# Attention scores from stacked high and low parts, and softmax work moved to ScalarE, in a two-layer hybrid encoder

## The chip, the cores and the metric

The kernel runs on one core of a Trainium2 chip. The core has TensorE (PE, the matrix unit; PEld in the profile is its loading of stationary operands), VectorE (DVE), ScalarE (ACT), GpSimd (POOL) and a queue that issues the transfers (SP). The metric is the device time of one execution in microseconds.

## The reference

```
for l in range(2):
    x = layer_norm(ALPHA*x + 0.5*swiglu_1(x));  x = layer_norm(ALPHA*x + mixer(x));  x = layer_norm(ALPHA*x + 0.5*swiglu_2(x))

mixer(x):                                  # x: 256 tokens x 1024
    sc_b, sc_c, sc_h, q, k, v, cc_a, cc_gate = split(x @ w_in)
    y_sc  = sc_b * dwconv3(sc_c * sc_h)
    q, k  = rope(q), rope(k)               # 8 query heads, 2 key/value heads, 64 columns each
    s     = q @ k.T / 8, where |i-j| <= 128, else -1e30
    m     = max(max(s), sink);  p = exp(s - m)
    y_att = (p @ v) / (sum(p) + exp(sink - m))
    y_cc  = silu(layer_norm(dwconv31(cc_a * sigmoid(cc_gate)) + b))
    return concat(y_sc, y_att, y_cc) @ w_out
```

All inputs and the output are float32.

## The kernel before

**Precision.** The large matmuls run in fp32r, a float32 form of less precision. Each operand is kept as a high part (the value rounded to fp32r, a ScalarE copy) and a low part (value minus high part, a subtraction on VectorE or GpSimd); `split` makes the two. A product is the sum of three matmuls, high-high, high-low and low-high (`mm3`). The attention's own matmuls, the scores and the product with v, and the transposes use plain float32 operands instead; the trace shows two matmul records for each float32 score matmul.

**Order.** The text of the kernel gives a program order. A scheduler then places each engine's instructions at compile time, by that order and by what it estimates to be ready; an engine runs its own list in the order that results. In the last part of the mixer (`in_order`) GpSimd's instructions keep the written order. Weights come in blocks of 128x2048: one DMA each, then a split. Blocks 7 to 11 of a mixer and the first four of the next feed-forward part have their subtractions on GpSimd.

**The mixer.** Tokens form two tiles t of 128. After the projections for the gated convolution, queries are projected (`proj_n`), rotated (`rotate`) and turned by four transposes per tile into qT[t] (`q_turned`, lines 538 to 543): partitions 0 to 63 hold the heads that use key head 0, partitions 64 to 127 those that use key head 1. Keys go the same way, one transpose per tile, into kT (128 x 256, `k_turned`). Values stay in vn. The long convolution is 62 taps on VectorE (`emit_conv`, line 572), handed out in portions by `fill(n)` between other work.

Softmax works on four units u: token tile u // 2, and half i = u % 2 of the heads, four heads at a time. For each unit
- `scores` (line 581) takes two PSUM banks of the pool acc (four banks) and computes for each c and each j a 64-row score matmul, on the partitions of key head j; then it adds the mask by a bf16 matmul with the identity;
- `exps` (592) takes maxima on VectorE, nm = -max, four exponentials on ScalarE with nm as bias and a summed output, and es = exp(sink + nm) by an addition on VectorE and one 128x4 exponential;
- `normalise` (608) adds es to the sums, inverts them and scales the probabilities on ScalarE;
- `p_turned` (616) transposes the probabilities and copies the two banks out, one on ScalarE (623), one on VectorE (625);
- `attend` (629) multiplies by v into one scratch bank (`tmp_bank`, four banks in this phase) and splits the result into y[i].

Around them run the remaining projections `proj_c`, 24 matmuls of 256 columns each per half (psc, psh, psb for the gated convolution), as the text below the functions lists: psc's first half, then turned queries and keys, psc's second half with the first scores inside it, and so on to the output projection `w_out2`. y[0] to y[3] are pairs of tiles (high, low) for the mixer's output; y[2] is written late by the gated convolution, y[3] by the Conformer part.

Of the kernel before, what the change touches and what calls it, by code (L numbers as in the profile page):

```python
# [8 lines left out]
F32 = mybir.dt.float32  # L9
F32R = mybir.dt.float32r  # L10
BF16 = mybir.dt.bfloat16
AF = mybir.ActivationFunctionType
ALU = mybir.AluOpType
# [3 lines left out]
P = 128  # L17
D = 1024
S = 256
# [3 lines left out]
KC = D // P  # L23
NG = DFF // 256
HD = 64
# [22 lines left out]
def encoder(ctx: ExitStack, tc: tile.TileContext, head_in, xt_in, x_in, w_in, gb_in, small_in, rope_in, out):  # L48
    nc = tc.nc
# [9 lines left out]
    mx = pool("mx", 1)  # L59
# [15 lines left out]
    def big():  # L75
        return hpool.tile([P, 512], F32, tag="big", bufs=6, name="big")
# [4 lines left out]
    def bank():  # L81
        return acc.tile([P, 512], F32, tag="acc", name="bank")
# [10 lines left out]
    def tmp_bank():  # L93
        return phase["pool"].tile([P, 512], F32, tag="mm", name="tmp")
# [58 lines left out]
    def use(k):  # L153
        i = state["use"]
        state["use"] += 1
        return tuple(t.rearrange("p (k n) -> p k n", k=k) for t in blocks.pop(i))

    def release(delay=2):
        tasks.append((state["tick"] + delay, emit_block))

    def fill(n):
        for _ in range(min(n, len(conv))):
            conv.pop(0)()

    def tick(parts=1):
        state["tick"] += 1
        while tasks and tasks[0][0] <= state["tick"]:
            tasks.pop(0)[1](parts)

    def mm3(ps, ah, al, bh, bl, first, last):  # L170
        nc.tensor.matmul(ps, ah, bh, start=first, stop=False)  # L171
        nc.tensor.matmul(ps, ah, bl, start=False, stop=False)  # L172
        nc.tensor.matmul(ps, al, bh, start=False, stop=last)  # L173

    def proj_c(ps, w, c, ks=range(KC)):
        cs = slice(c * P, (c + 1) * P)
        for k in ks:
            mm3(ps[:, c * S:(c + 1) * S], w[0][:, k, cs], w[1][:, k, cs], xT_h[:, k], xT_l[:, k], k == 0, k == KC - 1)
        if k == KC - 1:
            if c == 1:  # L180
                release()
            tick()
# [13 lines left out]
    def proj_n(ps, t, w, kh):  # L196
        for k in range(4):
            kk = kh * 4 + k
            nc.tensor.matmul(ps, xT_h[:, kk, t, :], w[0][:, k, :], start=kk == 0, stop=False)  # L199
            nc.tensor.matmul(ps, xT_h[:, kk, t, :], w[1][:, k, :], start=False, stop=False)  # L200
        for k in range(4):
            kk = kh * 4 + k
            nc.tensor.matmul(ps, xT_l[:, kk, t, :], w[0][:, k, :], start=False, stop=kk == KC - 1)  # L203
        if t == NT - 1:
            release()
        tick()
# [14 lines left out]
    def transpose(ps, srcs):  # L221
        for i, a in enumerate(srcs):
            nc.tensor.transpose(ps[:, i * P:(i + 1) * P], a, ident)  # L223
# [273 lines left out]
    def mixer(l, norm):  # L497
# [3 lines left out]
        b_cc, gb_cc, sink = sm[:, 68:70], sm[:, 70:74], sm[:, 74:82]  # L501
# [7 lines left out]
        nc.gpsimd.memset(upad, 0.0)  # L509
        ppad = mx.tile([P, 2, S + 2], F32, tag="ppad", name="ppad")  # L510
        nc.gpsimd.memset(ppad, 0.0)
        kT = mx.tile([P, S], F32, tag="kT", name="kT")
        half = HD // 2
        chan = lambda a: a.rearrange("p (c n) -> p c n", c=2)

        def rotate(t, src, n):
            src = src.rearrange("p (h d) -> p h d", d=HD)
            rf, r2f = big(), big()
            r, r2 = (a[:, 0:n * HD].rearrange("p (h d) -> p h d", d=HD) for a in (rf, r2f))
            bc = lambda a: a.unsqueeze(1).to_broadcast([P, n, a.shape[-1]])  # L520
            nc.vector.tensor_tensor(r, src, bc(rope[:, t, 0, :]), ALU.mult)
            nc.vector.tensor_tensor(r2[:, :, 0:half], src[:, :, half:HD], bc(rope[:, t, 1, 0:half]), ALU.mult)
            nc.vector.tensor_tensor(r2[:, :, half:HD], src[:, :, 0:half], bc(rope[:, t, 1, half:HD]), ALU.mult)
            nc.vector.tensor_tensor(r, r, r2, ALU.add)
            return rf

        def glu(ps):
            tg, u = big(), big()
            nc.scalar.activation(tg[:, 0:256], ps[:, 0:256], AF.Tanh, scale=0.5)
            nc.vector.scalar_tensor_tensor(u[:, 0:256], tg[:, 0:256], 1.0, ps[:, 256:512], op0=ALU.add, op1=ALU.mult)  # L530
            return u
# [3 lines left out]
            transpose(pt, [u[:, 0:P], u[:, P:2 * P]])  # L535
            nc.scalar.copy(upad[:, :, PAD + t * P:PAD + (t + 1) * P], chan(pt[:, 0:2 * P]))

        def q_turned(r):
            pq = tmp_bank()
            transpose(pq, [r[:, c * P:(c + 1) * P] for c in range(4)])  # L540
            q = mx.tile([P, 4, P], F32, tag="qT", bufs=2, name="qT")
            nc.scalar.copy(q.rearrange("p c n -> p (c n)"), pq)
            return q

        def k_turned(t, r):
            pk = tmp_bank()
            transpose(pk, [r[:, 0:P]])
            nc.scalar.copy(kT[:, t * P:(t + 1) * P], pk[:, 0:P])

        def kv(t, w):  # L550
            ps = tmp_bank()
            for k in range(KC):
                mm3(ps[:, 0:256], xT_h[:, k, t, :], xT_l[:, k, t, :], w[0][:, k, :], w[1][:, k, :], k == 0, k == KC - 1)
            v = mx.tile([P, P], F32, tag="vn", bufs=2, name="vn")
            nc.scalar.copy(v, ps[:, P:2 * P])
            r = rotate(t, ps[:, 0:P], 2)
            if t == 1:
                release()
            tick()
            return v, r  # L560
# [18 lines left out]
        y = [[hpool.tile([P, 2, S], F32R, tag=n, bufs=5, name="y" + n) for n in ("hh", "hl")] for _ in range(4)]  # L579

        def scores(t, i):
            mo = 1 - t
            scs = [chan(bank()) for _ in range(2)]
            for c in range(2):
                for j in range(2):
                    hp = slice(j * HD, (j + 1) * HD)
                    nc.tensor.matmul(scs[j][:, c, :], qT[t][hp, 2 * i + c, :], kT[hp, :], start=True, stop=False)
                for j in range(2):
                    nc.tensor.matmul(scs[j][:, c, mo * P:(mo + 1) * P], ident_b, mask[:, t, :], start=False, stop=True)
            return scs  # L590

        def exps(i, scs):
            hs = slice(4 * i, 4 * i + 4)
            den, mxs, nm, es = (st.tile([P, 4], F32, tag=n, name=n) for n in ("den", "mxs", "nm", "es"))
            pr = mx.tile([P, 4, S], F32, tag="pr", bufs=2, name="pr")
            for j in range(2):
                nc.vector.tensor_reduce(mxs[:, j::2], scs[j], AX.X, ALU.max)  # L597
            nc.vector.scalar_tensor_tensor(nm, mxs, -0.125, nsink[:, hs], op0=ALU.mult, op1=ALU.min)
            nc.vector.tensor_tensor(es, sink[:, hs], nm, ALU.add)
            for j in range(2):  # L600
                for c in range(2):
                    h = 2 * c + j
                    nc.scalar.activation(pr[:, h, :], scs[j][:, c, :], AF.Exp, bias=nm[:, h:h + 1], scale=0.125,
                                         accum_out=den[:, h:h + 1])
            nc.scalar.activation(es, es, AF.Exp)
            return pr, den, es

        def normalise(pr, den, es):
# [7 lines left out]
        def p_turned(pr):  # L616
            pTs = []
            for j in range(2):
                pp = bank()
                transpose(pp, [pr[:, 2 * c + j, kt * P:(kt + 1) * P] for kt in range(NT) for c in range(2)])  # L620
                pT = big()
                if j == 0:
                    nc.scalar.copy(pT, pp)
                else:
                    nc.vector.tensor_copy(pT, pp)
                pTs.append(pT)
            return pTs

# [43 lines left out]
        qT, vn, rk = [], [], []  # L672
        ga, q = bank(), bank()
# [6 lines left out]
        r0 = rotate(0, q, NH)  # L680
        ga, q = bank(), bank()
        proj_n(ga, 1, wga[0], 0)
        glu_turned(0, u0)
        proj_n(ga, 1, wga[1], 1)
        u1 = glu(ga)
        qT.append(q_turned(r0))
        proj_n(q, 1, wq[0], 0)
        glu_turned(1, u1)
        cacc = emit_conv()
# [2 lines left out]
        r1 = rotate(1, q, NH)  # L692
        wkv = use(KC)
        v, rk0 = kv(0, wkv)
        vn.append(v)
        fill(6)
        v, rk1 = kv(1, wkv)
        vn.append(v)
        psc = tmp_bank()
        wc = use(KC)  # L700
        fill(6)
        proj_c(psc, wc, 0)
        qT.append(q_turned(r1))
        k_turned(0, rk0)
        k_turned(1, rk1)
        prs, pTs = {}, {}

        def softmax(u, scs):
            prs[u] = exps(u % 2, scs)

        def S_(u):
            return scores(u // 2, u % 2)
# [8 lines left out]
            normalise(*prs[u])  # L721

        fill(5)
        proj_c(psc, wc, 1, range(4))
        softmax(0, S_(0))
        proj_c(psc, wc, 1, range(4, KC))
        scc = big()
        nc.scalar.copy(scc, psc)
        fill(9)
# [30 lines left out]
        scs = S_(3)  # L760
# [59 lines left out]
    for l in range(DEPTH):  # L820
        norm = ffn(l == 0, norm, False)
        norm = mixer(l, norm)
        norm = ffn(False, norm, l == DEPTH - 1)
# [85 lines left out]
```

## Time and profile before

| | |
|---|---|
| median of 3 runs | 932.67 us (932.43 to 933.49) |
| profiled execution | 932.76 us, span of its instructions 931.0 us |
| granted TensorE clock | 0.997 of 2.4 GHz |
| busy | PE 919.6, DVE 643.6, ACT 457.6, POOL 120.9 us |
| the two mixers' softmax stretches | about 225 to 262 and 684 to 722 us |

The span runs from the first to the last instruction of the profiled execution; the rest of the time lies around it. Busy shares are means over stages with different limits, so a stage is read from its own stretch. Matmuls overlap: their starts tell more than their durations.

### The profile page before, as it was taken

Reading aid. Unit: us, or ns where it says so; the run is one execution under the profiler, and the core shown is the slowest. Engines: PE = TensorE matmul, PEld = TensorE weight load, DVE = VectorE, ACT = ScalarE, POOL = GpSimd, SP = SyncE. Lnnn points to the kernel's source line nnn. Section 1 sums busy time; section 2 is a strip of 40 time slices with the busy share of each in tenths; the row PEclk is TensorE's granted clock in tenths of the full one; section 3 lists DMA queues with packets and bytes.
Section 4 is the critical chain, followed back from the end, with each engine's and each line's share of the span. In section 5 each row is a group of like instructions: output and inputs, shape, how many; then the busy total and the mean of one; then the engine's idle time right before and its main releaser. Section 6 shows DMA issues by size and latency. Waiting matters only on the chain.

```text
span 931.0 us, 12163 instructions
## 1 busy us (share of the span) xinstructions
PE 919.6 (99%) x4918; PEld 779.0 (84%) x4918; DVE 643.6 (69%) x815; ACT 457.6 (49%) x593; POOL 120.9 (13%) x112
## 2 busy tenths in 40 slices
PE   8999999999999999999999999999999999999996
PEld 6888888888788888888888888888887888888885
DVE  6966656689976766565777655667799766666546
ACT  5754444346744544445444444444456455444530
POOL 0010000007573000000000000000274610000000
PEclk9999999999999999999999999999999999999998
DMA  9966555536226655554456545543642376555301
GB/s 348 374 247 259 181 210 197 181 136 226 92 91 232 233 213 180 190 200 171 164 208 231 195 181 214 193 177 139 223 164 91 112 273 224 181 183 190 125 1 45
DMA packets 25976, 174.01 MB, mean 187 GB/s; under 512 B 2880, under 2 KB 3136, under 8 KB 5696
## 3 DMA queue, kind: packets, MB, share of 16 engines
q1 hardware_dynamic: 25920, 173.24, 51.4%
q8 instruction: 38, 0.62, 0.3%
q14 instruction: 18, 0.15, 0.0%
HBM read 172.18 MB, written 1.05 MB: 186 GB/s over the span
## 4 chain that ended last, share of the span: by engine, by line
PE 89%; DVE 7%; DMA 1%; POOL 1%; issue 1%; ACT 1%; DVEq 0%; POOLq 0%; ACTq 0%
PE wide L188 28%; PE wide L192 15%; PE bank L171 10%; PE bank L173 10%; PE bank L172 10%; PE bank L203 3%; PE bank L200 3%; PE bank L199 3%; DVE tmp L572 3%; PE bank L213 1%; PE tmp L223 1%; DVE mxs L597 1%; PE bank L223 1%; PE tmp L635 1%; PE bank L217 1%
## 5 line engine op out<-in xcount | busy, mean ns | idle before, releaser
L102 DVE TENSOR_TENSOR lo<-raw,hi 128x2048 fp32r<-128x2048 f32 (+2 forms) x175 | 316.9, 1825 | 212.1 <-ACT hi L101 212.0
L101 ACT CAST hi<-raw 128x2048 fp32r<-128x2048 f32 (+2 forms) x247 | 306.3, 1271 | 247.9 <-PE wide L188 154.3
L188 PE MATMUL wide<-xT,hi 128*128 128x512 f32 x1152 | 274.2, 390 | 0.0
L188 PEld LDWEIGHTS wide<-xT,hi 128*128 128x128 f32 x1152 | 214.0, 188 | 42.9
L192 PEld LDWEIGHTS wide<-xT,lo 128*128 128x128 f32 x1152 | 147.7, 191 | 5.6
L192 PE MATMUL wide<-xT,lo 128*128 128x256 f32 x1152 | 149.4, 283 | 0.0
L171 PE MATMUL bank<-hi,hh 128*128 128x512 f32 (+1 forms) x352 | 137.2, 390 | 0.0
L172 PE MATMUL bank<-lo,hh 128*128 128x512 f32 (+1 forms) x352 | 136.8, 389 | 0.0
L173 PE MATMUL bank<-hi,hl 128*128 128x512 f32 (+1 forms) x352 | 136.4, 387 | 0.0
L102 POOL TENSOR_TENSOR lo<-raw,hi 128x512 fp32r<-128x512 f32 x72 | 96.1, 1363 | 65.7 <-ACT hi L101 47.9
L252 POOL TENSOR_TENSOR rstd<-ve,mhalf 128x1 f32<-128x1 f32 x12 | 11.8, 985 | 661.5 <-DVE ve L251 661.5
L173 PEld LDWEIGHTS bank<-hi,hl 128*128 128x128 f32 x352 | 66.1, 188 | 13.9 <-DVE hl L102 0.2
L171 PEld LDWEIGHTS bank<-hi,hh 128*128 128x128 f32 x352 | 66.3, 188 | 12.8 <-ACT hh L101 0.4
L101 ACT CAST hh<-big 128x512 fp32r<-128x512 f32 x36 | 22.4, 621 | 110.6 <-DVE big L397 110.6
L172 PEld LDWEIGHTS bank<-lo,hh 128*128 128x128 f32 x352 | 66.3, 188 | 12.0
L199 PE MATMUL bank<-hi,xT 128*128 128x512 f32 x160 | 64.7, 404 | 0.1
L200 PE MATMUL bank<-lo,xT 128*128 128x512 f32 x160 | 62.7, 392 | 0.6 <-POOL lo L102 0.6
L405 DVE TENSOR_TENSOR big<-wide,big 128x512 f32<-128x512 f32 x72 | 49.2, 683 | 6.8 <-ACT big L404 6.8
L572 DVE SCALAR_TENSOR_TENSOR tmp<-upad,wc,tmp 128x256 f32<-128x256 f32 x116 | 49.7, 476 | 0.2
L404 ACT COPY big<-wide 128x512 f32<-128x512 f32 x72 | 42.3, 587 | 11.8 <-PE wide L192 11.5
L203 PE MATMUL bank<-hi,xT 128*128 128x512 f32 x160 | 43.0, 390 | 0.0
L102 DVE TENSOR_TENSOR hl<-big,hh 128x512 fp32r<-128x512 f32 x36 | 24.9, 692 | 24.0 <-ACT hh L101 24.0
(140 smaller groups left out, 897.0 us busy)
## 6 DMA issues: line engine op xcount, KB each, us to landing
raw<-in_w SPq DMA_DIRECT2D x152, 1024.0 KB, 4.8
gb<-in_gb SPq DMA_DIRECT2D x6, 1024.0 KB, 5.4
raw<-in_w SPq DMA_DIRECT2D x4, 512.0 KB, 7.8
head<-in_head SPq DMA_DIRECT2D x4, 384.0 KB, 4.1
raw<-in_w SPq DMA_DIRECT2D x4, 256.0 KB, 5.5
x<-in_x SPq DMA_DIRECT2D x2, 512.0 KB, 5.8
out<-x SPq DMA_DIRECT2D x4, 256.0 KB, 2.1
xraw<-in_xt SPq DMA_DIRECT2D x2, 256.0 KB, 5.8
```

Source lines behind the costliest of these rows:

```text
L101: nc.scalar.copy(hi, src)
L102: (eng or nc.vector).tensor_tensor(lo, src, hi.bitcast(F32), ALU.subtract)
L171: nc.tensor.matmul(ps, ah, bh, start=first, stop=False)
L172: nc.tensor.matmul(ps, ah, bl, start=False, stop=False)
L173: nc.tensor.matmul(ps, al, bh, start=False, stop=last)
L188: nc.tensor.matmul(ps[:, c], w[0][:, k, cs], xT[:, :, k], start=k == 0, stop=False)
L192: nc.tensor.matmul(ps[:, c, 0], w[1][:, k, cs], xT_h[:, k], start=False, stop=k == KC - 1)
L199: nc.tensor.matmul(ps, xT_h[:, kk, t, :], w[0][:, k, :], start=kk == 0, stop=False)
L200: nc.tensor.matmul(ps, xT_h[:, kk, t, :], w[1][:, k, :], start=False, stop=False)
L203: nc.tensor.matmul(ps, xT_l[:, kk, t, :], w[0][:, k, :], start=False, stop=kk == KC - 1)
L405: nc.vector.tensor_tensor(av, ps[:, :, 0], av, ALU.add)
L572: nc.vector.scalar_tensor_tensor(dst, upad[:, c, k:k + S], wc2[:, c, k:k + 1], part, op0=ALU.mult, op1=ALU.add)
```

## The change

Queries and keys are kept as high and low parts for the scores too. qT[t] becomes two 128-row tiles, one per key head j: the rows of head j hold the high part of its queries, the other 64 rows the low part of the same queries. They are stored in the still unused y[2 + t]. kT becomes four 128x256 tiles: for each j, part 0 holds the keys' high part on both halves of the rows, part 1 the low part on the rows of j and zeros (a GpSimd memset) on the others. Two fp32r matmuls of 128 rows give high-high plus low-high, then high-low. The mask matmul stands behind each head's two matmuls. Both token tiles' keys are transposed into one bank by one call. The second tile's query transposes are moved behind the first unit's scores, and six instead of four blocks of the running projection stand ahead of these. The sinks' exponentials are four 128x1 activations with nm as bias, without VectorE's addition, and both copies of turned probabilities run on ScalarE.

```diff
-        kT = mx.tile([P, S], F32, tag="kT", name="kT")
+        kT = mx.tile([P, 2, 2, S], F32R, tag="kT", name="kT")
...
-        def q_turned(r):
+        def q_turned(t, r):
             pq = tmp_bank()
             transpose(pq, [r[:, c * P:(c + 1) * P] for c in range(4)])
-            q = mx.tile([P, 4, P], F32, tag="qT", bufs=2, name="qT")
-            nc.scalar.copy(q.rearrange("p c n -> p (c n)"), pq)
-            return q
+            qs = [a.rearrange("p c n -> p (c n)") for a in y[2 + t]]
+            for j, q in enumerate(qs):
+                own, other = (slice(i * HD, (i + 1) * HD) for i in (j, 1 - j))
+                nc.scalar.copy(q[own], pq[own])
+                nc.vector.tensor_tensor(q[other], pq[own], q[own].bitcast(F32), ALU.subtract)
+            return [q.rearrange("p (c n) -> p c n", c=4) for q in qs]

-        def k_turned(t, r):
+        def k_turned(rs):
             pk = tmp_bank()
-            transpose(pk, [r[:, 0:P]])
-            nc.scalar.copy(kT[:, t * P:(t + 1) * P], pk[:, 0:P])
+            transpose(pk, [r[:, 0:P] for r in rs])
+            halves = [slice(j * HD, (j + 1) * HD) for j in range(2)]
+            for j, own in enumerate(halves):
+                nc.gpsimd.memset(kT[halves[1 - j], j, 1].bitcast(F32), 0.0)
+                nc.scalar.copy(kT[own, j, 0], pk[own, 0:S])
+                nc.vector.tensor_tensor(kT[own, j, 1], pk[own, 0:S], kT[own, j, 0].bitcast(F32), ALU.subtract)
+            for j, own in enumerate(halves):
+                nc.scalar.copy(kT[halves[1 - j], j, 0], pk[own, 0:S])
...
             for c in range(2):
                 for j in range(2):
-                    hp = slice(j * HD, (j + 1) * HD)
-                    nc.tensor.matmul(scs[j][:, c, :], qT[t][hp, 2 * i + c, :], kT[hp, :], start=True, stop=False)
-                for j in range(2):
+                    for part in range(2):
+                        nc.tensor.matmul(scs[j][:, c, :], qT[t][j][:, 2 * i + c, :], kT[:, j, part], start=part == 0, stop=False)
                     nc.tensor.matmul(scs[j][:, c, mo * P:(mo + 1) * P], ident_b, mask[:, t, :], start=False, stop=True)
...
-            nc.vector.tensor_tensor(es, sink[:, hs], nm, ALU.add)
...
-            nc.scalar.activation(es, es, AF.Exp)
+            for h in range(4):
+                nc.scalar.activation(es[:, h:h + 1], sink[:, 4 * i + h:4 * i + h + 1], AF.Exp, bias=nm[:, h:h + 1])
...
-                if j == 0:
-                    nc.scalar.copy(pT, pp)
-                else:
-                    nc.vector.tensor_copy(pT, pp)
+                nc.scalar.copy(pT, pp)
...
-        qT.append(q_turned(r1))
-        k_turned(0, rk0)
-        k_turned(1, rk1)
+        k_turned((rk0, rk1))
...
-        proj_c(psc, wc, 1, range(4))
+        proj_c(psc, wc, 1, range(6))
         softmax(0, S_(0))
-        proj_c(psc, wc, 1, range(4, KC))
+        qT.append(q_turned(1, r1))
+        proj_c(psc, wc, 1, range(6, KC))
```

## Rows read from the trace of the kernel before

**Rows 1.** The page, part 1: busy us, share of the span, instructions.

```profile
PE 919.6 (99%) x4918; PEld 779.0 (84%) x4918; DVE 643.6 (69%) x815; ACT 457.6 (49%) x593; POOL 120.9 (13%) x112
```

**Rows 2.** Busy times by stretch: length, then each engine's busy us, clock, DMA.

```profile
228.13:257.88 29.75, 29.48 (x209) 23.09 (x208) 29.69 (x76) 24.79 (x73) 15.96 (x14) 1.00 0.32 107
686.83:717.63 30.80, 30.50 (x209) 23.50 (x208) 30.69 (x77) 24.89 (x73) 15.27 (x12) 1.00 0.29 103
```

**Rows 3.** Timeline of PE, turned queries to first scores: start, us, instruction.

```profile
222.51 0.60 PE L223 MATMUL tmp<-ident,big 128*128 128x128 f32 x4
222.86 0.36 PE L171 MATMUL tmp<-xT,hi 128*128 128x256 f32 x1
...
223.78 0.33 PE L223 MATMUL tmp<-ident,big 128*128 128x128 f32 x1
223.87 0.36 PE L171 MATMUL tmp<-xT,hi 128*128 128x256 f32 x1
224.07 0.28 PE L172 MATMUL tmp<-xT,hi 128*128 128x256 f32 x1
...
224.87 0.28 PE L171 MATMUL tmp<-xT,hi 128*128 128x256 f32 x1
224.99 0.28 PE L172 MATMUL tmp<-xT,hi 128*128 128x256 f32 x1
225.20 0.70 PE L587 MATMUL bank<-kT,qT 64*128 64x256 f32 x4
...
226.69 0.29 PE L589 MATMUL bank<-mask,ident_b 128*128 128x128 bf16 x2
226.78 0.36 PE L173 MATMUL tmp<-xT,lo 128*128 128x256 f32 x1
226.98 0.28 PE L171 MATMUL tmp<-xT,hi 128*128 128x256 f32 x1
```

**Rows 4.** Timeline of PE, a later attend of layer one and score call of layer two.

```profile
246.56 1.09 PE L635 MATMUL tmp<-big,vn 128*64 128x256 f32 x8 [0.27 <-DVE den L609]
...
696.65 1.42 PE L587 MATMUL bank<-kT,qT 64*128 64x256 f32 x4
```

**Rows 5.** DVE's groups, 205 to 262 us: count, busy us, mean ns, idle before.

```profile
L599 DVE TENSOR_TENSOR es<-small,nm 128x4 f32<-128x4 f32 x4 | 3.1, 766 | 0.0
L625 DVE COPY big<-bank 128x512 f32<-128x512 f32 x4 | 2.7, 677 | 0.0
...
L102 DVE TENSOR_TENSOR yhl<-tmp,yhh 128x256 fp32r<-128x256 f32 x4 | 1.6, 408 | 0.0
```

**Rows 6.** ACT's groups in the same stretch.

```profile
L623 ACT COPY big<-bank 128x512 f32<-128x512 f32 x4 | 2.4, 597 | 0.1
...
L548 ACT COPY kT<-tmp 128x128 f32<-128x128 f32 x2 | 0.5, 266 | 0.8 <-PE tmp L223 0.8
```

**Rows 7.** Timeline of ACT at the end of the first unit's exponentials.

```profile
230.49 0.49 ACT L603 ACTIVATE pr<-bank,nm 128x256 f32<-128x256 f32 x1
230.85 0.22 ACT L603 ACTIVATION_READ_ACCUMULATOR pr<-bank,nm 128x1 f32 x1
230.94 0.22 ACT L605 ACTIVATE es<-es 128x4 f32<-128x4 f32 x1
231.04 1.15 ACT L101 CAST hi<-raw 128x512 fp32r<-128x512 f32 x2
```

**Rows 8.** Waits, 205 to 262 us: who for whom, total, times, longest.

```profile
ACT pr L603 <- DVE nm L598: 2.3, 2, 1.3
...
ACT pr L614 <- DVE den L610: 1.4, 1, 1.4
```

**Rows 9.** Timeline of POOL, start of the kernel.

```profile
1.75 0.53 POOL L511 MEMSET ppad<- 128x516 f32 x1
```

**Rows 10.** Timelines of ACT and DVE at the first token tile's keys.

```profile
216.95 0.27 ACT L555 COPY vn<-tmp 128x128 f32<-128x128 f32 x1 [0.65 <-PE tmp L173]
...
217.25 0.29 DVE L521 TENSOR_TENSOR big<-tmp,rope 128x128 f32<-128x128 f32 x1
```

More of the change, by code (lines that the diff above doesn't have):

```diff
@@ L685, in mixer @@
         u1 = glu(ga)
-        qT.append(q_turned(r0))
+        qT.append(q_turned(0, r0))
         proj_n(q, 1, wq[0], 0)
```

## Prediction

> **What bounds the kernel now.** I read the views from the outside in. The page's busy times come first: TensorE (PE) works through 99% of the span [rows 1], so time can only be won by giving it less to do, or by taking back the few places where it waits. Then come the busy times by stretch, for the part of each layer's mixer in which scores, softmax and the last projections run [rows 2]. There PE, VectorE (DVE) and ScalarE (ACT) are all near their limit: of 29.75 us in the first layer PE is busy 29.48, DVE 29.69 and ACT 24.79. The reader is to see that ACT, the engine that the change loads, has 29.75 - 24.79 = 4.96 us free per layer there, no more. Then PE's instructions in order of time, whose starts give the real price of each: neighbouring 256-column projection matmuls start 0.12 us apart, as those at 224.87 and 224.99 [rows 3]. Last the waits of PE that hide inside its busy time [rows 4], and those of ACT [rows 8].
>
> **The scores on TensorE.** One call of scores() is issued between two projection matmuls that start at 224.99 and 226.98 [rows 3]. Of these 1.99 us two projection spacings of 0.12 belong to the projection, so a call costs 1.75 us; there are eight (four units in two layers). The new call has, for each of two pairs of heads and each head of the pair, two fp32r matmuls of 128 rows by 256 columns and then one mask matmul. The fp32r matmuls have the shape and type of the projection's, so I give them its 0.12 us. For a mask the rows give a spacing of (226.78 - 226.69)/2 = 0.045, and the first fp32r matmul behind masks takes 226.98 - 226.78 = 0.20 and not 0.12, so leaving them costs 0.08. A call of the new kind leaves the masks four times (the old one twice), since the mask now stands behind each head: 4 x (0.24 + 0.045 + 0.08) = 1.46 us. That saves 0.29 us per call, 2.3 us over eight. No row shows fp32r going over into bf16, so both ends are kept: if the passage out of a mask costs nothing, a call is 4 x 0.285 = 1.14 and eight save 4.9; if going in costs as much as going from projection to scores does now (225.20 - 224.99 - 0.12 = 0.09), a call is 4 x 0.455 = 1.82 and eight lose 0.6. I take the middle, which is what rows show of leaving a mask.
>
> **Keys turned together.** The two key transposes are now two visits of PE among projection matmuls. One starts at 223.78; the projection goes on 0.09 later, and its first matmul takes 224.07 - 223.87 = 0.20 in place of 0.12 [rows 3]: 0.17 us for the visit. Transposes standing together start (222.86 - 222.51)/4 = 0.0875 apart, so one visit with two of them is 2 x 0.0875 + 0.08 = 0.255. That saves 0.34 - 0.255 = 0.085 per layer; I take 0.2 for both layers. The ends are nothing and 0.5, if a pause that now stands ahead of a visit goes too. The four query transposes stay as they are; the second tile's are only moved behind the first scores.
>
> **VectorE.** It loses, per layer, four additions for the sinks (3.1 us together, 0.77 each [rows 5]) and four copies of probabilities (2.7 us). It gains four query differences of 512 columns, at 0.68 like that copy, and two key differences of 256 columns at 0.41: 3.5 us. Net it is 2.3 us lighter per layer. This is worth nothing by itself: most of what remains are convolution taps, which fill DVE until about the last score and whose result is used late. It does shorten the queue ahead of the softmax's small steps.
>
> **ScalarE.** It gains four copies of 0.60 per layer [rows 6] and three more exponentials per unit. Columns cost (0.597 - 0.266)/384 = 0.86 ns each by the two copies of rows 6. An exponential with a per-row bias is followed by the next start after 230.85 - 230.49 = 0.36 us [rows 7]; less 256 columns (0.22) that leaves 0.14 for one of a single column. The old one, without such a bias, holds ACT for 231.04 - 230.94 = 0.10 though it lasts 0.22, so neighbours overlap by 0.12. Sinks: 4 x 0.14 - 0.10 = 0.46 per unit, 1.8 per layer (0.3 and 1.34 per unit, if they cost 0.10 or the full 0.36). Copies: 4 x (0.60 - 0.12) = 1.9. Together 3.7 us of the 4.96 free, with ends at 3.1 and 7.3. The doubled query copies (about 0.5 more per tile, half the partitions but all columns) and the key copies (four of 256 columns for two of 128, about 0.8 more) lie ahead of the softmax, where ACT still waits for matmuls. So ACT goes from 24.8 to 28.5 us in a stretch that PE would like to shorten to about 28.9. It is covered, with little left; without that cover each us more on ACT is a us on PE.
>
> The Trainium skill (ScalarE: Activation LUTs, "What ACT_TABLE_LOAD costs") speaks against this part: it gives an activation with a per-partition bias pointer about 280 ns before its columns, some 93 ns of them overlapped with the neighbour. By it the sinks would be an estimated 4 x 0.19 - 0.10 = 0.66 us per unit and ACT's addition about 4.5 us per layer, which nearly closes the gap. The 0.48 us that the wide exponential lasts fits that figure; its spacing fits the smaller one, and the sum goes by the spacing.
>
> **Memsets and waits.** The two new GpSimd memsets of the key tile need no place in GpSimd's queue near the scores: the memset of ppad, written at the head of the mixer, ran at 1.75 us of the span [rows 9], so the schedule pulls such work forward. Were it not so, they would stand behind the weight splits. PE's hidden waits now are of two kinds: a score call whose bank waits for exponentials (its first step takes 1.42 us in place of 0.70), and an attend whose bank waits (0.27) [rows 4]. There are two of each in the two layers, 1.75 us together. A lighter DVE takes some away: 1.0, my choice between nothing and all. New waits: the first score now needs key halves that pass ACT and DVE in turn, and the next projection's bank waits for the query's two copies and two differences. I put 1.0 us on these in both layers together, between nothing and the second rival's 3.7.
>
> **Sum.** The profiled execution took 932.76 us (span 931.0, the rest around it). -2.3 - 0.2 - 1.0 + 1.0 = -2.5. It stands 0.09 above the median of the runs shown, so I forecast 930.2, 0.27% less.
>
> **Rivals.** *First, on the other side: ACT becomes the bound.* ACT now waits 2.3 us for the maxima and 1.4 for the denominators per layer [rows 8]. These are dependencies, not spare time. If all 3.7 stayed, the stretch would need 28.5 + 3.7 = 32.2 us for 29.75, 2.5 more per layer, 5.0 in all; less 0.2 for the keys that is 937.5. With a third left (1.2) it is 29.7, as before: 932.3. From 2.4 us left on, the kernel is slower by more than 0.2%. For it: three engines are full there. Against it: a lighter DVE brings maxima and denominators sooner, and weight casts in that stretch can be done later.
> *Second: the query tile holds the free bank.* Scratch has four PSUM banks; two carry the convolution and one the running projection. DVE starts to read the key bank only once ACT has copied from it (217.25 after 216.95 + 0.27 [rows 10]). The query's bank is thus held for 2 x (0.60 + 0.68) = 2.6 us, while only six matmuls, 0.72 us, of the running projection are left. The next one waits 0.6 (its predecessor's bank emptied by one copy) to 1.8 us per layer, 1.2 to 3.7 in all beside the forecast's 1.0: some 932. Against it: the second score call, 1.46 us, may be issued into the gap.
> *Third: the change doesn't make the scores cheaper.* Passing in and out of bf16 four times costs the upper end, a loss of 0.6 in place of the gain of 2.3: 933.1. For it: the old order kept the masks together, and the old heads of a pair ran side by side on halves of the array.
>
> **How the numbers follow.** Forecast 0.50, ACT 0.20 (three fifths of it slower by over 0.2%), bank 0.15, scores 0.15. Two tenths of a per cent, 1.9 us here, is about what can be told from no change. Faster by more: the forecast's cases but a few, 0.48. Within: the remainder of them, the bank, the scores and the mild form of the ACT rival, 0.38. Slower: 0.14. The likeliest case alone spans 928.0 to 931.6. The range is 927.6 (scores at their lower end, 2.6 under the forecast) to 934.2, past the bank and the scores' upper end and half way into the ACT rival.
>
> **What would show it.** Right: score matmuls about 0.12 us apart and under 1.5 us per call; key transposes together; ACT near 28 us in the stretch with waits for the maxima shorter than now; no wait of PE over 0.5 us there. Wrong: masks over 0.2 us each time; PE waiting for an exponential or a probability copy; a gap in PE behind the moved query transposes; a first score later than the keys' projection allows.

## The result, and the profile after

The changed kernel takes 938.33 us (median of six runs, 936.76 to 940.01) where the kernel before took 932.95 in the same session (six runs, 932.31 to 933.77). The ratio is 1.0059, with a 95% interval of 1.0049 to 1.0068: slower by 0.59%, 5.4 us. The forecast was 930.2 with a range up to 934.2, so both its sign and its range were wrong.

The profiled execution took 938.33 us with a span of 936.5. Part 1 of its page, to be read beside [rows 1]:

```profile
PE 921.1 (98%) x4918; PEld 783.2 (84%) x4918; DVE 642.8 (69%) x811; ACT 470.3 (50%) x633; POOL 122.0 (13%) x116
```

PE is busy 1.5 us longer, where cheaper scores should have made it shorter, and it is idle for 936.5 - 921.1 = 15.4 us where it was 931.0 - 919.6 = 11.4. VectorE (DVE) was to lose 2.3 us per layer, and lost 0.8 over the whole kernel. The scores themselves are as forecast. This is PE's timeline in layer one, to compare with [rows 3]:

```profile
224.81 0.28 PE L172 MATMUL tmp<-xT,hi 128*128 128x256 f32 x1
224.93 0.47 PE L598 MATMUL bank<-kT,yhh 128*128 128x256 f32 x2
225.24 0.23 PE L599 MATMUL bank<-mask,ident_b 128*128 128x128 bf16 x1
225.28 0.50 PE L598 MATMUL bank<-kT,yhl 128*128 128x256 f32 x2
...
226.35 0.23 PE L599 MATMUL bank<-mask,ident_b 128*128 128x128 bf16 x1
226.42 0.61 PE L223 MATMUL tmp<-ident,big 128*128 128x128 f32 x4
226.78 0.36 PE L173 MATMUL tmp<-xT,lo 128*128 128x256 f32 x1
226.98 0.40 PE L598 MATMUL bank<-kT,yhh 128*128 128x256 f32 x2
```

A call lasts from 224.93 to 226.42, 1.49 us, where 1.46 was put and the old one took 1.75. No gap stands ahead of it, nor behind the moved query transposes at 226.42. The loss is later. These are PE's waits (who waits for whom, total us, times, longest):

```profile
PE tmp L642 <- DVE yhl L102: 4.1, 4, 2.2
PE bank L200 <- POOL lo L102: 1.7, 4, 0.5
PE tmp L331 <- DVE big L327: 1.2, 1, 1.2
PE bank L171 <- ACT big L632: 0.4, 2, 0.2
```

The longest is an attend of layer one (line 642) that waits for its scratch bank, which VectorE empties by the low part of the attend before it (yhl, line 102). PE's timeline there, and then the windows of the same stretch (window: length, busy us of PE, PEld, DVE, ACT and POOL, granted clock, DMA share, GB/s):

```profile
249.51 0.40 PE L172 MATMUL bank<-lo,yhh 128*128 128x512 f32 x1
252.12 1.77 PE L642 MATMUL tmp<-big,vn 128*64 128x256 f32 x8 [2.21 <-DVE yhl L102]
```

```profile
250.00:254.00 4.00, 1.88 (x9) 0.89 (x10) 4.00 (x12) 2.62 (x13) 0.71 (x2) 0.80 0.72 264
254.00:258.00 4.00, 4.00 (x14) 3.21 (x15) 4.00 (x13) 4.00 (x11) 2.28 (x2) 0.77 0.01 2
```

PE stands for 2.21 us, and behind that the granted clock is down (0.80 and 0.77 of full speed over 4 us each, a mix of its two levels of 2.4 and 1.2 GHz, so 0.20 x 4 + 0.23 x 4 = 1.7 us worth of full clock is not granted), where before it was 1.00 [rows 2]. VectorE is busy through all of both windows. What it does while PE waits:

```profile
246.19 0.41 DVE L102 TENSOR_TENSOR yhl<-tmp,yhh 128x256 fp32r<-128x256 f32 x1
246.52 3.17 DVE L759 TENSOR_SCALAR big<-ppad,small 128x256 f32<-128x256 f32 x2
249.61 1.66 DVE L761 SCALAR_TENSOR_TENSOR big<-ppad,small,big 128x256 f32<-128x256 f32 x4
251.19 0.15 DVE L608 SCALAR_TENSOR_TENSOR nm<-mxs,nsink 128x4 f32<-128x4 f32 x1
251.26 0.48 DVE L583 SCALAR_TENSOR_TENSOR tmp<-upad,wc,tmp 128x256 f32<-128x256 f32 x1
251.66 0.41 DVE L102 TENSOR_TENSOR yhl<-tmp,yhh 128x256 fp32r<-128x256 f32 x1
```

The low part at 251.66 stands behind six products of the gated convolution (lines 759 and 761). The first two of them last 3.17 us together. In the kernel before they lasted 0.34 and 0.31:

```profile
246.41 0.34 DVE L753 TENSOR_SCALAR big<-ppad,small 128x256 f32<-128x256 f32 x1
...
246.76 0.31 DVE L753 TENSOR_SCALAR big<-ppad,small 128x256 f32<-128x256 f32 x1
```

And GpSimd (POOL) in the changed kernel subtracts for the weight splits through just that time; before, it ran no subtraction between 243.90 and 251.46:

```profile
244.90 0.67 POOL L555 MEMSET kT<- 64x256 f32 x2 [3.69 <-issue]
245.53 3.74 POOL L102 TENSOR_TENSOR lo<-raw,hi 128x512 fp32r<-128x512 f32 x3
```

Ahead of the three subtractions stand the memsets of the key tile for layer two, behind the last scores of layer one, which read the same tile. Layer two has no such memsets in that place. Up to the products, the scores, ScalarE's casts and VectorE's steps stand there as in layer one, 463.6 us later. GpSimd, VectorE and PE then go on like this:

```profile
708.19 3.81 POOL L102 TENSOR_TENSOR lo<-raw,hi 128x512 fp32r<-128x512 f32 x3 [3.38 <-ACT hi L101]
...
710.13 2.03 DVE L759 TENSOR_SCALAR big<-ppad,small 128x256 f32<-128x256 f32 x2
...
714.59 1.09 PE L642 MATMUL tmp<-big,vn 128*64 128x256 f32 x8 [1.07 <-DVE yhl L102]
```

The subtractions come 0.95 us sooner by that measure, the products take 1.14 us less, PE waits 1.07 us in place of 2.21, and the granted clock stays at 1.00. The two layers share the loss unequally: from the first score to the first residual addition behind the mixer, layer one takes 50.1 us (224.93 to 275.04) where it took 45.4 (225.20 to 270.59), and layer two 47.4 (688.51 to 735.88) where it took 46.5 (683.90 to 730.35).

So the first reading is: VectorE's queue is late, and it is late because instructions in it last as long as GpSimd works beside them. What the trace alone can't say is which part of the change makes it so.

### The profile page after: what moved, and what is told of

Its sections match the earlier page's. It is cut to its first block, busy times and chain, and to the rows that moved or that the text cites. A ratio compares the mean times of both kernels' runs of the same rounds, so it can differ in the third digit from the quotient of the medians.

```text
span 936.5 us, 12196 instructions
## 1 busy us (share of the span) xinstructions
PE 921.1 (98%) x4918; PEld 783.2 (84%) x4918; DVE 642.8 (69%) x811; ACT 470.3 (50%) x633; POOL 122.0 (13%) x116
## 4 chain that ended last, share of the span: by engine, by line
PE 93%; DVE 5%; POOL 1%; issue 1%; ACT 0%; DVEq 0%; POOLq 0%
PE wide L188 28%; PE wide L192 15%; PE bank L173 10%; PE bank L171 10%; PE bank L172 9%; PE bank L203 3%; PE bank L200 3%; PE bank L199 3%; PE tmp L171 2%; PE tmp L172 2%; PE tmp L173 2%; PE tmp L223 1%; PE bank L213 1%; PE bank L223 1%; PE bank L598 1%; PE tmp L642 1%
## 5 line engine op out<-in xcount | busy, mean ns | idle before, releaser
L404 ACT COPY big<-wide 128x512 f32<-128x512 f32 x72 | 42.3, 587 | 12.5 <-PE wide L192 12.2
```

## The experiments

The expectations name their theories by a letter. The first four runs weighed **Q** (VectorE's order: the products stand ahead of the last unit's maxima and the low part, and meet GpSimd's splits, which come later because ScalarE's added work delays the casts that they wait for), **A** (ScalarE's load itself is the bound) and **S** (the turned queries and keys cost more than the scores save). Later ones define theirs. Every kernel was timed in five rounds beside the kernel before; medians of the latter were 933.33, 933.52, 933.63 and 933.43 us in the four sessions. Where a run is set against the changed kernel, the differences of both to the kernel before of their own session are compared (5.4 us for the changed kernel).

**The two parts of the change, each alone.** `scores_only` takes the changed kernel and puts the sinks' additions and the second probability copy back on VectorE; `act_only` takes the kernel before and does those two edits alone:

```diff
-            nc.vector.tensor_tensor(es, sink[:, hs], nm, ALU.add)
...
-            nc.scalar.activation(es, es, AF.Exp)
+            for h in range(4):
+                nc.scalar.activation(es[:, h:h + 1], sink[:, 4 * i + h:4 * i + h + 1], AF.Exp, bias=nm[:, h:h + 1])
...
-                if j == 0:
-                    nc.scalar.copy(pT, pp)
-                else:
-                    nc.vector.tensor_copy(pT, pp)
+                nc.scalar.copy(pT, pp)
```

> The scores' part alone: high and low parts, keys turned together, the moved query transposes; the sinks' addition and the second probability copy are back on VectorE. Theory Q (VectorE's queue: the fourth unit's nm and the second attend's low part stand behind the gated convolution's products, which GpSimd's late weight splits stretch because ScalarE's added work makes the weight casts late): with ScalarE relieved the casts come earlier, the products run in about 0.65 us, TensorE's wait before the third attend goes, and the scores' 0.26 us per call show: about 930.5 us. Theory A (ScalarE's load itself is the bound): the same, 930 to 931. Theory S (moved queries and keys cost more than the scores save): still slower than before, 935 to 938.

> The kernel before with only the two moves to ScalarE: sinks' exponentials with bias, both probability copies. Theory Q: the casts come late, the products collide with GpSimd, 935 to 938 us if they meet as in the changed kernel, 932 to 934 if they miss each other. Theory A: 936 to 938 wherever the products stand. Theory S: 932 to 933.

`scores_only` took 939.97 us (ratio 1.0071, 1.0059 to 1.0084) and `act_only` 933.93 (1.0010, 1.0002 to 1.0019). The first lies outside what each of the three allowed; the loss belongs to the scores' part. A falls, and so does the half of Q that blames ScalarE's moves: the loss is there without them.

**The products out of the way, and the probability copy back.** `products_late` is the changed kernel with the loop of lines 754 to 762 written behind `softmax(3, scs)`; `after_pt_dve` is the changed kernel with the second probability copy on VectorE again.

> The whole change, with the gated convolution's six products written behind the fourth unit's softmax instead of ahead of it. Theory Q: nm of the fourth unit and the second attend's low part come about 3 us sooner on VectorE in layer one, 2 us in layer two; TensorE's waits of 2.2 and 1.1 us before the third attend go, and with them the stretch at the lower clock: 932 to 934 us. Theory A: ScalarE has the same work, 937 to 938. Theory S: 937 to 938.

> The whole change, but the second copy of turned probabilities stays on VectorE. ScalarE loses about 1.9 us per layer. Theory Q: the gain depends on whether the casts come early enough for GpSimd to be through before the products: 931 to 936 us. Theory A: half of the loss comes back, 934 to 936. Theory S: 938.

`products_late` took 935.96 us (1.0032, 1.0020 to 1.0043): 2.8 us come back, not all, and less than Q allowed. VectorE's timeline shows why, and GpSimd's beside it:

```profile
247.95 0.41 DVE L102 TENSOR_TENSOR yhl<-tmp,yhh 128x256 fp32r<-128x256 f32 x1
248.28 2.77 DVE L608 SCALAR_TENSOR_TENSOR nm<-mxs,nsink 128x4 f32<-128x4 f32 x1
250.98 2.04 DVE L583 SCALAR_TENSOR_TENSOR tmp<-upad,wc,tmp 128x256 f32<-128x256 f32 x5
252.94 0.41 DVE L102 TENSOR_TENSOR yhl<-tmp,yhh 128x256 fp32r<-128x256 f32 x1
```

```profile
247.29 3.75 POOL L102 TENSOR_TENSOR lo<-raw,hi 128x512 fp32r<-128x512 f32 x3
```

With the products gone, the next step in the queue takes their place: an instruction over four columns (nm) lasts 2.77 us, to 251.05, and GpSimd's three subtractions end at 251.04. `after_pt_dve`, with less on ScalarE and more on VectorE, took 948.22 (1.0166, 1.0152 to 1.0180), the worst of all and outside what each of the three allowed. That points away from ScalarE and to VectorE.

**The differences on VectorE.** `no_differences` is the changed kernel without the six differences per layer, `before_plus_differences` the kernel before with such differences added, `q_old_place` undoes the move of the second query turn and `taps_products_late` changes VectorE's order.

```diff
-                nc.vector.tensor_tensor(q[other], pq[own], q[own].bitcast(F32), ALU.subtract)
+                nc.gpsimd.memset(q[other].bitcast(F32), 0.0)
...
-                nc.vector.tensor_tensor(kT[own, j, 1], pk[own, 0:S], kT[own, j, 0].bitcast(F32), ALU.subtract)
+                nc.gpsimd.memset(kT[own, j, 1].bitcast(F32), 0.0)
```

> The changed kernel, in which GpSimd writes zeros where VectorE would write the low parts of queries and keys: six differences per layer (3.5 us) less on VectorE, and all copies, score matmuls and places as they are. The low parts are left out of the scores. Theory D (what costs is VectorE's added time ahead of and within the softmax, in a stretch where VectorE was already full): about 931 against 933.3, that is the forecast's gain of 2 to 2.5, and no wait of PE over 1 us for a low part or for the maxima. Rival P (the new place and order of the second query turn and the first scores costs): still 937 to 939. Rival S (the doubled copies on ScalarE cost): still 937 to 939.

> The kernel before, with differences that nothing reads added behind the copies of the turned queries and keys: per tile two of 512 columns on 64 rows and two of 128 columns, 3.8 us more of VectorE's time per layer, and nothing else. Theory D: 937 to 940 against 933.3, with waits of PE for low parts or maxima as in the changed kernel. Rivals P and S: 933 to 934.

> The changed kernel with the second tile's queries turned ahead of the keys again, and the first scores behind four matmuls of the projection in place of six. Theory D: 938 within 1.5, since VectorE has the same work. Rival P: 933 or less. Rival S: 937 to 939.

> The changed kernel with the gated convolution's six products written behind the last unit's softmax, and the eleven taps that were written among the last three units left to the end, where the rest of the taps are written. VectorE has the same work in another order. Theory D in the form that its order makes the waits: the low part of the second attend and the last softmax come in time, no wait of PE over 1 us for them, and 932 to 934. If VectorE's sum is the cost, whatever the order: 936 as with the products alone moved, the wait then standing at the turn of the convolution (PE waiting for the taps).

`no_differences` took 929.94 us (0.9961, 0.9948 to 0.9973): without the differences the change is worth 3.6 us, though all copies on ScalarE are kept, so S falls. (The zeros are twelve more memsets on GpSimd.) `before_plus_differences` took 944.09 (1.0111, 1.0095 to 1.0127), which by its sign speaks for D but is more than D expected. Two of its waits of PE name another cause for part of it:

```profile
PE tmp L223 <- DVE yhl L545: 2.3, 2, 1.2
...
PE tmp L223 <- DVE yhh L554: 1.7, 2, 0.9
```

There the key transposes wait for a scratch bank that the added differences hold, 4.0 us in all, which the changed kernel doesn't show. So this run prices no difference cleanly. `q_old_place` took 940.85 (1.0073, 1.0060 to 1.0085): the old place is no better (it is 2.0 us worse, a little more than D allowed), and P falls. `taps_products_late` took 936.43 (1.0033, 1.0021 to 1.0044): moving the taps as well gains nothing over moving the products alone, as its second reading had it.

**Sum or place.** `fewer_taps` takes 3.2 us per layer of other work from VectorE (`if 1 <= k <= 4: continue` in the loop that queues the taps); `no_key_differences` takes the keys' share of the differences; `scores_no_differences` is `scores_only` without the six differences; `parts_on_halves` is another layout, shown below.

> The changed kernel without eight of the 62 convolution taps of each layer (the second to fifth of each channel chunk), 8 x 0.40 = 3.2 us less of VectorE's time per layer, all differences kept; part of the convolution is left out. Theory D in the form that VectorE's sum up to the last scores is what costs, whosever work it is: 930 to 933 against 933.3. Rival K (the differences cost by their place, as links between a turned bank and the scores, not by their time): 936 to 939.

> The changed kernel with zeros from GpSimd for the low parts of the keys alone; the queries' differences stay. 0.85 us less on VectorE per layer, all of it ahead of the first scores. Theory D: 936 to 937.5, a fifth to a third of the way from 938.3 to 929.9. Rival K (the chain to the first scores costs): 932 or less.

> The scores' part alone (sinks' addition and second probability copy on VectorE as before) with zeros from GpSimd in place of the six differences per layer; the low parts are left out of the scores. VectorE has the same work as in the kernel before, TensorE the cheaper scores. Theory D: 930 to 933, and slower than the run with ScalarE's moves and no differences (929.9) if those moves help VectorE. Rival M (the moves to ScalarE bring nothing): the same as that run within 0.6.

> A version with less VectorE work: high and low parts kept on the rows of their head as in the kernel before, three fp32r matmuls of 64 rows per head (high by high, low by high, high by low) with the two heads of a pair in turn. One difference of 512 columns on 128 rows per query tile and one of 256 for the keys, 1.8 us per layer in place of 3.5, and half the query copies on ScalarE; the rest as changed. If the two heads' matmuls run side by side on halves of the array, a score call costs 6 x 0.12 + 0.25 = 1.0 us and theory D gives 928 to 932; if they run one after the other, 12 x 0.12 + 0.25 = 1.7 us, the old price, and theory D gives 932 to 935.

`fewer_taps` took 933.78 us (1.0002, 0.9993 to 1.0010), 5.2 less than the changed kernel, just above D's range and below K's; its attend still waits the same 2.21 us. `no_key_differences` took 938.42 (1.0047, 1.0034 to 1.0059), 0.6 less for 0.85 us per layer, which is no gain clear of the noise and a miss for D as for K. `scores_no_differences` took 940.31 (1.0074, 1.0061 to 1.0087): by D it should have been faster than the kernel before, because VectorE's own work is the same by count and PE's is less. It is 6.7 us slower. That overturned D as a matter of instructions alone, and part 1 of its page says where to look:

```profile
PE 920.4 (98%) x4918; PEld 781.9 (83%) x4918; DVE 652.7 (70%) x815; ACT 462.3 (49%) x601; POOL 125.6 (13%) x128
```

VectorE runs 815 instructions, as before [rows 1], and is busy 652.7 us where it was 643.6. As many instructions of the same kinds, in another order, last 9.1 us longer.

**GpSimd's subtractions taken away.** In three kernels GpSimd's weight splits are left out, so that nothing of VectorE's can meet them.

```diff
-            args = hi[:, cs], lo[:, cs], raw[:, cs], nc.gpsimd if i in POOL_BLOCKS else None
+            args = hi[:, cs], lo[:, cs], raw[:, cs], i in POOL_BLOCKS
...
-        (eng or nc.vector).tensor_tensor(lo, src, hi.bitcast(F32), ALU.subtract)
+        if not eng:
+            nc.vector.tensor_tensor(lo, src, hi.bitcast(F32), ALU.subtract)
...
-        blocks[i] = (hi, lo)
+        blocks[i] = (hi, hi if i in POOL_BLOCKS else lo)
```

> The kernel before without GpSimd's weight splits: for the blocks whose low parts GpSimd makes, the matmuls read the high part twice, so those low parts are left out. It is the control of the next two runs: nothing of VectorE's can stand behind a GpSimd subtraction in the mixer. Theory C (what makes VectorE late is its steps between SBUF tiles that stand behind GpSimd's subtractions): some gain, 927 to 932. Rival N (VectorE's own work and order alone): 932 to 934.

> The changed kernel without GpSimd's weight splits in the same way. Theory C: the loss of 5.4 against its control goes, and it is 0 to 3 us faster than the control. Rival N: 3.5 to 6 us slower than the control, as with the splits.

> The scores' part alone, without the differences and without GpSimd's weight splits: VectorE's own work is that of the control, TensorE's score calls are cheaper. Theory C: 1 to 3 us faster than the control, where the same kernel with GpSimd's splits was 6.7 slower than the kernel before. Rival N: 5 to 7 us slower than the control.

| | with GpSimd's splits, us | against before | without them, us | against the control |
|---|---|---|---|---|
| kernel before | 933.43 | | 929.15 (928.74 to 929.44), control | |
| changed kernel | 938.33 | +5.4 | 929.26 (928.97 to 929.59) | +0.1 |
| scores' part without differences | 940.31 | +6.7 | 930.72 (930.35 to 931.35) | +1.6 |

The differences in the third column are to the kernel before of each run's own session (932.95 and 933.63 us in the lower two rows).

The loss of 5.4 us is 0.1 and that of 6.7 is 1.6. N falls. C holds for the loss, but not for the gain that it promised: the changed kernel is no faster than its control. PE's own waits for GpSimd's low parts go with the splits too, so this run doesn't tell them from VectorE's delay; the list of waits does, with 1.7 us for the former and 4.1 for the latter. VectorE's order in this stretch of the changed kernel is the same without the splits; only the durations differ:

```profile
246.10 0.42 DVE L103 TENSOR_TENSOR yhl<-tmp,yhh 128x256 fp32r<-128x256 f32 x1
246.43 0.61 DVE L760 TENSOR_SCALAR big<-ppad,small 128x256 f32<-128x256 f32 x2
246.95 1.67 DVE L762 SCALAR_TENSOR_TENSOR big<-ppad,small,big 128x256 f32<-128x256 f32 x4
248.54 0.16 DVE L609 SCALAR_TENSOR_TENSOR nm<-mxs,nsink 128x4 f32<-128x4 f32 x1
248.61 0.48 DVE L584 SCALAR_TENSOR_TENSOR tmp<-upad,wc,tmp 128x256 f32<-128x256 f32 x1
249.00 0.42 DVE L103 TENSOR_TENSOR yhl<-tmp,yhh 128x256 fp32r<-128x256 f32 x1
```

The two products take 0.61 us in place of 3.17, the low part starts at 249.00 in place of 251.66, and the granted clock of 250 to 258 us is 1.00.

**A version that beats both.** `parts_on_halves` keeps high and low parts on the rows of their head. One difference of 128 rows then serves a whole query tile, and one the keys.

```diff
-            for j, q in enumerate(qs):
-                own, other = (slice(i * HD, (i + 1) * HD) for i in (j, 1 - j))
-                nc.scalar.copy(q[own], pq[own])
-                nc.vector.tensor_tensor(q[other], pq[own], q[own].bitcast(F32), ALU.subtract)
+            nc.scalar.copy(qs[0], pq)
+            nc.vector.tensor_tensor(qs[1], pq, qs[0].bitcast(F32), ALU.subtract)
...
+                for a, b in ((0, 0), (1, 0), (0, 1)):
+                    for j in range(2):
+                        hp = slice(j * HD, (j + 1) * HD)
+                        nc.tensor.matmul(scs[j][:, c, :], qT[t][a][hp, 2 * i + c, :], kT[hp, b], start=a == b, stop=False)
```

It took 930.54 us (0.9968, 0.9955 to 0.9980). PE's timeline of its first score call:

```profile
224.68 0.39 PE L592 MATMUL bank<-kT,yhh 64*128 64x256 f32 x2
224.90 0.28 PE L592 MATMUL bank<-kT,yhl 64*128 64x256 f32 x2
225.02 0.28 PE L592 MATMUL bank<-kT,yhh 64*128 64x256 f32 x2
225.23 0.28 PE L594 MATMUL bank<-mask,ident_b 128*128 128x128 bf16 x2
...
226.12 0.61 PE L223 MATMUL tmp<-ident,big 128*128 128x128 f32 x4
```

The two heads' matmuls run side by side (0.12 us for the middle pair, 0.21 to 0.22 for the pairs next to other kinds of matmul), and the call costs 226.12 - 224.68 = 1.44 us, no more than the stacked form's 1.49, for half of the differences. The step of 1.0 that was put as the lower case was too low: it had 0.25 for all masks and passages. The version also does without the memsets and with half of the query copies on ScalarE, so its gain can't be put down to the differences alone.

## Why the prediction was wrong

**The scores and the keys: right.** 1.49 us per call for 1.46, the key transposes in one visit, no gap ahead of the first scores. Without GpSimd's splits PE's busy sum shows the gain: 918.3 us in the control and 916.1 in the changed kernel, 2.2 less for a forecast of 2.3 and 0.2.

**VectorE: the step that failed.** The prediction called it "2.3 us lighter per layer" and found that "worth nothing by itself", as taps whose result is used late would cover any change. Both halves were wrong. First the size. The sinks' addition was taken at its mean of 0.77 us [rows 5]. Its minimum, median and maximum (ns) in the kernel before, and then in the control without GpSimd's splits, are:

```profile
L599 DVE TENSOR_TENSOR es<-small,nm x8: 148/864/1123, 229.0 to 711.7; 128x4 f32<-128x4 f32 x8
```

```profile
L600 DVE TENSOR_TENSOR es<-small,nm x8: 151/153/158, 229.0 to 708.7; 128x4 f32<-128x4 f32 x8
```

Four fifths of that row was not work of the addition but time behind GpSimd's subtractions. Removing the addition removes 0.15 us of work; the rest can pass to the next such step (nm, the products). By this price the part is -4 x 0.15 - 2.7 + 3.5 = +0.2 us per layer, not -2.3. The busy sums without splits agree in kind: 631.1 us in the control, 632.4 in the changed kernel.

Second the cover. In a stretch where VectorE was busy 29.69 of 29.75 us [rows 2], its order counts, not only its sum. The low parts and negated maxima stand among taps and products, and PE waits for them. In place of the 1.0 us put on new waits in both layers, PE waits 4.1 us for low parts (2.21 of them once) and 1.1 more for GpSimd's low parts in the following stage (1.7 against 0.6 by the list of waits), and the clock is lower behind the long wait. Nor do the taps cover VectorE's sum: `fewer_taps`, with 3.2 us per layer less of just these taps, still has the 4.1 us of waits and takes 5.2 us less than the changed kernel.

**The memsets: read from the first layer only.** The prediction saw the memset of ppad at 1.75 us and held that the schedule pulls such work forward. That is the memset of layer one; layer two's ran at 248.71, in the middle of layer one's mixer, in the kernel before, and layer two's key memsets in the changed kernel came at 244.90, ahead of the weight splits. By the difference between the layers, taken as theirs alone, they cost an estimated 2.8 us of the 5.4: 2.21 - 1.07 = 1.1 of wait, and from nm to the residual addition 23.85 us in layer one (251.19 to 275.04) against 22.22 in layer two (713.66 to 735.88), where the clock stayed up. This is read from one trace; no run moves the memsets alone. They are not the whole cause: in `scores_only` layer two's memsets stand behind the splits (at 245.60, where four subtractions last from 239.17 to 244.20), its two layers take 49.0 and 49.1 us by the same measure, and it loses 6.6 us.

**ScalarE: the first rival, wrong.** ScalarE's moves alone are worth +0.1% and relieve VectorE: without the differences the kernel takes 929.94 us with them and 940.31 without. They hold ScalarE longer than the prediction's sum had it:

```profile
243.13 0.87 ACT L615 ACTIVATE es<-small,nm 128x1 f32<-128x1 f32 x4
243.87 1.68 ACT L101 CAST hi<-raw 128x512 fp32r<-128x512 f32 x3
```

The four start to the cast's start is 0.74 us, 0.185 for each where 0.14 was put. The Trainium skill (ScalarE: Activation LUTs, "What ACT_TABLE_LOAD costs") gave the estimate of 0.19, and here the trace agrees with it.

**The bank (second rival) and the scores' price (third): not seen.** The second score call was issued into the gap, as the prediction held possible. A version of the bank's wait did appear where the added differences held it in the kernel before (`before_plus_differences`).

**What stays open.** Without GpSimd's splits PE gains 2.2 us of busy time and gives it back in small waits (0.8 for low parts, 0.8 for ScalarE's casts in a later stage, and some of 0.2), so the change is worth nothing there, and the scores' part without differences is still 1.6 us slower than its control. Which meeting moves when an instruction is added or taken is not predicted by any theory here: 0.85 us less per layer gave 0.6 us, within the noise, 3.2 less gave 5.2, and 3.5 less gave 9.0.

## What to carry to other kernels

A mean duration far above the minimum of the same instruction is no price: look at minimum and maximum, and ask what the engine stood behind, because that wait can stay when the instruction goes and fall on the next. Where an in-order engine is full through a stretch, read its order there, and count each instruction that the edit puts ahead of a step for which another engine waits. Where a row shows when an instruction runs, look for its copy in the next layer, and for what stands behind that copy in its queue. Where a split into high and low parts is needed, lay it out so that one instruction over all 128 rows does it: a difference over 64 rows took 0.69 us here for 512 columns, as long as a 128-row copy of 512 columns (0.68).

## What the runs showed of the hardware

Only some of VectorE's instructions last longer beside GpSimd's subtractions. Those with one operand in PSUM kept their time (taps of 0.48, low parts of an attend of 0.41 us in every kernel above); those between SBUF tiles alone can last longer: 0.31 to 2.9 us for a product with a scalar, 0.15 to 2.77 for nm. They don't each time: the rotation's addition of 128x128 (line 524) took 1.17 us at 218.10 and 0.28 at 221.61 in the kernel before, both while GpSimd subtracted. Taking GpSimd's splits away took 12.5 us off VectorE's busy sum in the kernel before (643.6 to 631.1), 10.4 in the changed one (642.8 to 632.4) and 21.9 in the scores' part without differences (652.7 to 630.8), with the same instructions in each pair. The Trainium skill (SBUF — State Buffer, "Who interferes with whom") states it as a rule: a VectorE instruction with two SBUF inputs, or one in a two-port mode, excludes a GpSimd instruction that reads SBUF, and the one that comes second is blocked for the whole of the other's. The traces agree for the steps named here. One VectorE step can stand through two or three subtractions in turn (2.77 us, where one of them lasts 3.74 / 3 = 1.25).
